# A hybrid decoder step on one core: a first stage of six column tiles with its first rows in single transfers, and a tail that adds the residual on TensorE

## The chip, the core and the metric

The kernel runs on one core of a Trainium2 chip. The metric is device time in microseconds of one execution; lower is better. A time of a kernel is the median of several runs. Besides these runs there is one profiled execution, and every row below is from that one.

The core has TensorE (PE in the rows; its weight load is PEld), VectorE (DVE), ScalarE (ACT), GpSimd (POOL) and SyncE (SP). Each works through its own queue in order. Transfers are issued here from the queues of SP, ACT and POOL.

## The reference

One layer of a hybrid decoder on 280 token columns: 16 meta tokens, 256 prompt tokens and 8 running sequences with one new token each. All data is fp32. Cut to its frame:

```python
u = rmsnorm(h, pre_mix_g)
mix, conv, ssm, ret = mixers(u, ...)     # u @ w_in, conv, Mamba-2 heads, retention heads
h = h + rmsnorm(mix @ w_out, post_mix_g)
f = rmsnorm(h, pre_ffn_g)
f = (silu(f @ w_gate) * (f @ w_up)) @ w_down
h = h + rmsnorm(f, post_ffn_g)           # y_prompt, y_sample
```

`rmsnorm` is x * rsqrt(mean(x*x) + eps) * g. The model width is 2048, or 16 tiles of 128 rows. The outputs are the new h and the new convolution, SSM and retention states.

## The kernel before

Tokens lie on the free axis and features on the partitions, so a projection is a product of 128x128 weight blocks with the 280 (later 264) token columns. To get fp32 accuracy from the faster fp32r mode, weights and activations are split into a high part rounded to fp32r and a low remainder. A block then takes three matmuls (`three`, L129 to L133): high by high, high by low, low by high.

Weights stream in chunks of eight blocks, 512 KB each (`Stream.block`, L112 to L125). SP issues the load into `raw`, four buffers; ScalarE casts to `hi` (L122) and VectorE subtracts to get `lo` (L123), three buffers each. The first chunk is cut in four.

The first stage, `gemm("xb", uin0, ..., outer=4)` at L336, runs with the row tile k outside and four column tiles inside: dt, two tiles of B and the first of C. Each has its own PSUM bank. While it runs, `prep` (L163 to L178) brings in the rows of x on the same SP queue, two at a time (the first two apart), multiplies them by the norm weight `g_pre` from the parameter table `pps`, splits them into `uh` (ScalarE) and `ul` (VectorE, L171), squares them (ScalarE) and adds the squares into `xsum` on GpSimd (L178). The parameter table comes by ScalarE's queue. Nine dummy matmuls (`WARM`) run before the first data is there.

When the stage ends, `const_loads` loads the constants from GpSimd's queue; this is paced by a tiny copy that reads the `ul` of row 11. Then `token_norms` sums `xsum` over the partitions (`pr`, L208) and makes the norm `rbc` on ScalarE and VectorE. Every finished column tile is scaled by it out of PSUM; dt goes through some twenty VectorE operations (`do_dt`), the others through the convolution (`do_xbc`, three VectorE operations L321 of 304 columns each). Column tiles 4 to 12 follow one by one, with k inside. After tiles 7, 8 and 9 a further piece of `do_dt` runs: its transposes, the cumulated decay `lcd`, which is written to DRAM and read back into all partitions as four tiles `lcb` (L293 to L296), and the differences `wj` that read these (L304). The projections k, q, v, z, g, the output projection `o`, the two FFN gemms `f` and `d` follow.

The tail: gemm `d` leaves 16 rows `p` (times the norm weight) and sums of squares; `rstds` makes the norm from them with an fp32 ones-matmul (L638) and ScalarE's Ln and Exp. Then for each of eight pairs of rows one multiplication by the norm (L895) and one addition of the residual `hr` (L903), shared between VectorE and GpSimd, and one store (L904), alternating between SP and ScalarE. `hr` comes back from DRAM in eight loads issued behind gemm d.

The framework puts the instructions of every queue in order before the run: it plays the program through with its own estimates of durations and takes the ready instruction of highest priority. Priority is program order; `tc.high_priority(offset=n)` moves an instruction up by n, and `keep_in_program_order` fixes its place. The order stays, whatever the run's own durations are.

Of the kernel before, what the change touches and what calls it, by code (L numbers as in the profile page):

```python
# [7 lines left out]
F32 = mybir.dt.float32  # L8
F32R = mybir.dt.float32r
# [38 lines left out]
WARM = 9  # L48
OUTF = 6


@with_exitstack
def hybrid_step(ctx: ExitStack, tc: tile.TileContext, wall, xT, pp, cc, dmask, cs, convst, ssm, ret,
# [32 lines left out]

    pps = cp.tile([P, NPP], F32, name="pps")
# [41 lines left out]
    def three(ps, xhi, xlo, first, last):  # L129
        hi, lo = stream.block()  # L130
# [27 lines left out]
    xs = [slot(f"x{i}") for i in range(4)]  # L158
    uh = [slot(f"uh{i}", dt=F32R) for i in range(4)]
    ul = [slot(f"ul{i}", dt=F32R) for i in range(4)]  # L160
    xsum = slot("xsum", NA, 2)

    def prep(k):  # L163
        i, j = divmod(k, 4)
        with tc.high_priority(offset=1500):
            for q in (j, j + 1):
                if k == 0 or q == j:
                    n = 1 if k == 0 else 2
                    nc.sync.dma_start(xs[i][:, q:q + n, :], xT[:, 4 * i + q:4 * i + q + n, :])
                A.activation(uh[i][:, q, :], xs[i][:, q, :], AF.Copy, scale=par("g_pre", 4 * i + q))  # L170
                V.scalar_tensor_tensor(ul[i][:, q, :], xs[i][:, q, :], par("g_pre", 4 * i + q),  # L171
                                       uh[i][:, q, :].bitcast(F32), MULT, SUB)
            if k == 0:
                A.activation(xsum, xs[i][:, j:j + 2, :], AF.Square)
            else:
                sq = slot(f"xq{k}", NA, 2)
                A.activation(sq, xs[i][:, j:j + 2, :], AF.Square)
                G.tensor_tensor(xsum, xsum, sq, ADD)  # L178

    ready = set()  # L180

    def uin0(k, n):
        if k % 2 == 0 and k not in ready:
            ready.add(k)
            prep(k)
        return uin(k, n)

    def uin(k, n):
        i, j = divmod(k, 4)
        return uh[i][:, j, NA - n:NA], ul[i][:, j, NA - n:NA]  # L190
# [26 lines left out]

    def pinned(out, in_):
        tc.keep_in_program_order(G.dma_start(out, in_))
# [660 lines left out]
    o2 = [slot(f"p{i}", NO) for i in range(4)]  # L880
    ev, sums = ev_norm(o2, "g_pffn")
# [3 lines left out]
    hrs = []  # L885
    for k in range(0, KT, 2):
        hr = slot(f"hr{k}", NO, 2)
        load(hr, hd[:, k:k + 2, :])
        hrs.append(hr)
    pool_mul, pool_add = (7,), (0, 2, 4, 7)  # L890

    def scaled(n):
        ok = o2[n // 2][:, 2 * (n % 2):2 * (n % 2) + 2, :]
        e = G if n in pool_mul else V
        e.tensor_tensor(ok, ok, rstd.unsqueeze(1).to_broadcast([P, 2, NO]), MULT)  # L895

    scaled(7)
    for n in range(8):
        ok = o2[n // 2][:, 2 * (n % 2):2 * (n % 2) + 2, :]
        if n < 7:  # L900
            scaled(n)
        e = G if n in pool_add else V
        e.tensor_tensor(ok, ok, hrs[n], ADD)  # L903
        (nc.sync if n % 2 == 0 else nc.scalar).dma_start(yT[:, 2 * n:2 * n + 2, :], ok)  # L904
# [49 lines left out]
def _layout(i):  # L954
# [4 lines left out]
    first = np.concatenate([np.tile(dt, (1, 8)), bb, cm[:, :128]], 1)  # L959
    wo, wd = i["w_out"][0], i["w_down"][0]  # L960
    gu = np.stack([i["w_gate"][0].reshape(DM, FT, P), i["w_up"][0].reshape(DM, FT, P)], 2).reshape(DM, 2 * DFF)
    seq = [_blocks(first, 1), _blocks(np.concatenate([cm[:, 128:], xx], 1)), _blocks(k), _blocks(q), _blocks(v),
           _blocks(z), _blocks(g), _blocks(wo[:, :512], 1), _blocks(wo[:, 512:]), _blocks(gu[:, :P * OUTF], 1),
           _blocks(gu[:, P * OUTF:]), _blocks(wd)]
    wall = np.concatenate(seq, 0)
    wall = np.ascontiguousarray(wall.reshape(-1, CB, P, P).transpose(0, 2, 1, 3)).reshape(-1, P, CB * P)
    xtok = np.concatenate([i["meta_tokens"], i["x_prompt"][0], i["x_sample"][:, 0]], 0)
# [16 lines left out]
    return [wall, xT, pp, c, d, cs, convst, ssm, ret]  # L984
# [31 lines left out]
```

## Time and profile before

| | us |
|---|---|
| median of 3 runs | 1280.14 |
| lowest, highest | 1277.64, 1282.41 |
| the profiled execution | 1281.71 |
| its span in the profile | 1279.9 |

The span is the part of the profiled execution from its first to its last instruction; 1.8 us lie around it. The profiled execution took 1.57 us more than the median. PE carries 98% of the span, and the chain of work that ended last lies on PE for 95%. A matmul row's duration contains the time in which its columns drain while the next is already streaming in, so the distance between two starts is what one more matmul costs. The clock column is the granted clock of TensorE: 1.00 is 2.4 GHz and 0.50 is 1.2 GHz.

### The profile page before, as it was taken

What the parts mean: (1) busy time and instruction counts of PE and PEld (TensorE: products, weight loads), DVE (VectorE), ACT (ScalarE), POOL (GpSimd) and SP (SyncE); (2) the same over time, 40 slices, a digit from 0 to 9 for tenths busy, and PEclk for the clock granted to TensorE, in tenths of its full rate; (3) what the DMA queues carried; (4) which work ended last, traced back from release to release, by engine and by line L of the source; (5) the groups of instructions that cost most, each with busy time, mean ns of one, the idle gap of its engine ahead of it and who ended that gap; (6) DMA issues with size and microseconds to landing.
All of it is one profiled execution on the core that took longest, in us unless ns stands there. A gap on an engine that the chain in (4) does not pass through costs nothing.

```text
span 1279.9 us, 24519 instructions
## 1 busy us (share of the span) xinstructions
PE 1254.4 (98%) x10078; PEld 1240.9 (97%) x10078; DVE 821.3 (64%) x1247; ACT 607.8 (47%) x826; POOL 153.1 (12%) x218
## 2 busy tenths in 40 slices
PE   8989999999999999999999999999999999999994
PEld 7989999999999999999999999999999999999994
DVE  7978779984775458566666666666666544444445
ACT  6665434445854446544444444444444433333331
POOL 3320001100001221101110110101101000000013
PEclk9999999999999999999999999999999999999997
DMA  8656347774466556577677766767676555555562
GB/s 271 206 190 215 121 147 260 273 260 144 136 214 230 182 180 217 183 244 245 229 236 247 246 231 231 248 215 248 214 247 229 183 181 181 182 182 181 181 223 93
DMA packets 74768, 266.41 MB, mean 208 GB/s; under 512 B 8528, under 2 KB 9440, under 8 KB 74656
## 3 DMA queue, kind: packets, MB, share of 16 engines
q1 hardware_dynamic: 60192, 214.17, 51.7%
q0 software_dynamic: 13744, 49.52, 10.7%
q8 instruction: 79, 1.29, 0.4%
q10 hardware_dynamic: 720, 1.16, 0.2%
q14 instruction: 33, 0.27, 0.1%
HBM read 246.15 MB, written 18.66 MB: 207 GB/s over the span
## 4 chain that ended last, share of the span: by engine, by line
PE 95%; DMA 2%; DVE 1%; issue 1%; SPq 0%; ACT 0%; POOL 0%; DVEq 0%; ACTq 0%
PE f L131 13%; PE f L133 13%; PE f L132 13%; PE d L132 7%; PE d L131 7%; PE d L133 7%; PE o L131 2%; PE o L132 2%; PE o L133 2%; PE xb L132 1%; PE xb L133 1%; PE xb L131 1%; PE k L131 1%; PE v L131 1%; PE v L132 1%; PE k L132 1%
## 5 line engine op out<-in xcount | busy, mean ns | idle before, releaser
L123 DVE TENSOR_TENSOR lo<-raw,hi 128x1024 fp32r<-128x1024 f32 (+1 forms) x405 | 492.3, 1217 | 357.8 <-ACT hi L122 353.1
L122 ACT CAST hi<-raw 128x1024 fp32r<-128x1024 f32 (+1 forms) x405 | 422.1, 1043 | 601.9 <-PE f L132 191.7
L131 PE MATMUL f<-fh,hi 128*128 128x264 f32 x1408 | 400.6, 285 | 0.0
L133 PE MATMUL f<-fh,lo 128*128 128x264 f32 x1408 | 399.3, 284 | 0.0
L132 PE MATMUL f<-fl,hi 128*128 128x264 f32 x1408 | 398.6, 283 | 0.0
L132 PEld LDWEIGHTS f<-fl,hi 128*128 128x128 f32 x1408 | 264.8, 188 | 0.3 <-issue 0.2
L131 PEld LDWEIGHTS f<-fh,hi 128*128 128x128 f32 x1408 | 264.8, 188 | 0.3 <-DVE f L863 0.2
L133 PEld LDWEIGHTS f<-fh,lo 128*128 128x128 f32 x1408 | 264.6, 188 | 0.0
L132 PE MATMUL d<-al,hi 128*128 128x264 f32 x704 | 200.2, 284 | 0.0
L131 PE MATMUL d<-ah,hi 128*128 128x264 f32 x704 | 199.7, 284 | 0.0
L133 PE MATMUL d<-ah,lo 128*128 128x264 f32 x704 | 199.4, 283 | 0.0
L131 PEld LDWEIGHTS d<-ah,hi 128*128 128x128 f32 x704 | 132.5, 188 | 0.0
L132 PEld LDWEIGHTS d<-al,hi 128*128 128x128 f32 x704 | 132.4, 188 | 0.0
L133 PEld LDWEIGHTS d<-ah,lo 128*128 128x128 f32 x704 | 132.3, 188 | 0.0
L131 PE MATMUL o<-mh,hi 128*128 128x264 f32 x256 | 72.8, 284 | 0.0
L132 PE MATMUL o<-ml,hi 128*128 128x264 f32 x256 | 72.6, 284 | 0.0
L133 PE MATMUL o<-mh,lo 128*128 128x264 f32 x256 | 72.4, 283 | 0.0
L869 POOL COPY pace<-f 128x1 f32<-128x1 f32 x25 | 28.6, 1144 | 362.2 <-DVE f L863 362.2
L858 DVE TENSOR_TENSOR f<-f,rhc 128x264 f32<-128x264 f32 x88 | 37.6, 432 | 49.1 <-PE f L133 48.8
L131 PE MATMUL xb<-uh,hi 128*128 128x280 f32 x208 | 61.8, 299 | 3.1 <-ACT hi L122 3.1
L133 PE MATMUL xb<-uh,lo 128*128 128x280 f32 x208 | 61.1, 297 | 3.4 <-DVE lo L123 3.4
L132 PE MATMUL xb<-ul,hi 128*128 128x280 f32 x208 | 61.7, 297 | 1.2 <-DVE ul L171 1.2
(296 smaller groups left out, 1983.2 us busy)
## 6 DMA issues: line engine op xcount, KB each, us to landing
raw<-in_dram SPq DMA_DIRECT2D x401, 512.0 KB, 3.6
rs<-in_dram POOLq DMA_DIRECT2D x16, 512.0 KB, 5.3
su<-in_dram POOLq DMA_DIRECT2D x16, 512.0 KB, 4.9
out_dram<-su POOLq DMA_DIRECT2D x16, 512.0 KB, 3.9
hb<-in_dram POOLq DMA_DIRECT2D x8, 512.0 KB, 5.9
hu<-in_dram POOLq DMA_DIRECT2D x8, 512.0 KB, 5.1
out_dram<-hu POOLq DMA_DIRECT2D x8, 512.0 KB, 4.1
lcb<-lcd POOLq DMA_DIRECT2D x4, 544.0 KB, 9.1
```

Of the source, the lines that this page charges most:

```text
L122: A.copy(self.hi[:, f:f + w], raw[:, f:f + w])
L123: V.tensor_tensor(self.lo[:, f:f + w], raw[:, f:f + w], self.hi[:, f:f + w].bitcast(F32), SUB)
L131: T.matmul(ps, hi, xhi, start=first, stop=False)
L132: T.matmul(ps, hi, xlo, start=False, stop=False)
L133: T.matmul(ps, lo, xhi, start=False, stop=last)
L858: V.tensor_tensor(t, ps, rhc, MULT)
L869: tc.keep_in_program_order(G.tensor_copy(pace, t[:, 0:1]))
```

## The change

The first stage takes six column tiles at once (dt, two of B, two of C, the first of x) in place of four, with four banks of one PSUM pool and two of the other. The weights are laid out for that.

For its first four row tiles, the 16 norm weights, the 280 columns of x and the six weight blocks lie next to each other in one new input `head`: 1064 numbers per partition and row tile, 545 KB. SP loads each of the four into a buffer of its own; the first in two parts, the first part with the norm weights, x and two blocks (552 numbers, 283 KB). `bring` casts and splits from there.

The other rows of x come from GpSimd's queue, two per load, each load paced by a tiny copy that reads the `ul` of four rows before (for rows 4 to 7, of rows 0 and 1). The squares are summed on VectorE. `WARM` is 7.

In the tail GpSimd does nothing. VectorE multiplies all eight pairs by the norm. For the first four pairs TensorE adds: an fp32 matmul of the identity with the residual opens a bank, another with the scaled row closes it, and ScalarE copies the sum out. VectorE adds the other four pairs. SP issues all stores. The residual comes in four loads that stand ahead of gemm d.

```diff
-WARM = 9
+WARM = 7
+OUTX = 6
+NHEAD = 4
+HX = 16
+HW = HX + NA + OUTX * P
+NPE = 4
...
-                    w = CB * P // (4 if c == 0 else 1)
-                    for f in range(0, CB * P, w):
-                        nc.sync.dma_start(raw[:, f:f + w], wall[c, :, f:f + w])
-                        A.copy(self.hi[:, f:f + w], raw[:, f:f + w])
-                        V.tensor_tensor(self.lo[:, f:f + w], raw[:, f:f + w], self.hi[:, f:f + w].bitcast(F32), SUB)
+                    nc.sync.dma_start(raw, wall[c])
+                    A.copy(self.hi, raw)
+                    V.tensor_tensor(self.lo, raw, self.hi.bitcast(F32), SUB)
...
+    def x_load(k, after):
+        if k % 4 == 0:
+            xs[k // 4] = slot(f"x{k // 4}")
+        pace = cp.tile([P, 1], F32, name=f"pacex{k}")
+        i, j = divmod(after, 4)
+        tc.keep_in_program_order(G.tensor_copy(pace, ul[i][:, j, 0:1].bitcast(F32)))
+        pinned(xs[k // 4][:, k % 4:k % 4 + 2, :], xT[:, k:k + 2, :])
+    heads = []
+    for k in range(NHEAD):
+        heads.append(slot(f"head{k}").rearrange("p a n -> p (a n)"))
+        with tc.high_priority(offset=1500):
+            cut = HX + NA + 2 * P if k == 0 else HW
+            for f0, f1 in ((0, cut), (cut, HW)):
+                if f0 < f1:
+                    tc.keep_in_program_order(nc.sync.dma_start(heads[k][:, f0:f1], head[k, :, f0:f1]))
+    def bring(k):
...
+            if k == 0:
+                V.tensor_copy(hi[:, :cut], w[:, :cut])
+                parts(k, x, g)
+                V.tensor_tensor(lo[:, :cut], w[:, :cut], hi[:, :cut].bitcast(F32), SUB)
...
+            else:
+                A.copy(hi[:, :cut], w)
+                parts(k, x, g)
+                V.tensor_tensor(lo[:, :cut], w, hi[:, :cut].bitcast(F32), SUB)
...
+            x_load(2 * k + NHEAD, k) if k < 2 else None
     def prep(k):
...
+            squares(k, xs[i][:, j:j + 2, :])
+            if k + 4 < KT:
+                x_load(k + 4, k)
...
-    gemm("xb", uin0, KT, NA, 0, 4, ev_first, outer=4, before=const_loads)
-    for m in range(4, 13):
-        gemm("xb", uin, KT, NA, m, m + 1, ev_first, pool=pm if m < 6 else pg)
+    for k in range(KT):
+        ws = bring(k) if k < NHEAD else [None] * OUTX
+        if k >= NHEAD and k % 2 == 0:
+            prep(k)
+        xh, xl = uin(k, NA)
+        for ps, w in zip(pss, ws):
+            three(ps[:, :NA], xh, xl, k == 0, k == KT - 1, w)
+    const_loads()
+    for m, ps in enumerate(pss):
+        ev_first(m, ps[:, :NA])
+    for m in range(OUTX, 13):
+        gemm("xb", uin, KT, NA, m, m + 1, ev_first, pool=pm if m == OUTX else pg)
...
+    for i in range(4):
+        hr = slot(f"hr{i}", NO)
+        load(hr, hd[:, 4 * i:4 * i + 4, :])
...
+    def residual(k):
+        sums_[k] = bank(f"h{k}", NO) if k % 2 else pg.tile([P, 512], F32, name=f"h{k}", tag="g")[:, :NO]
+        T.matmul(sums_[k], ident, hrs[k // 4][:, k % 4, :], start=True, stop=False)
+    for k in range(4):
+        residual(k)
+    for n in range(NPE):
+        scaled(n)
+        for k in (2 * n, 2 * n + 1):
+            ok = o2[k // 4][:, k % 4, :]
+            T.matmul(sums_[k], ident, ok, start=False, stop=True)
+            A.copy(ok, sums_.pop(k))
+        store(n)
+        for k in (2 * n + 4, 2 * n + 5):
+            if k < 2 * NPE:
+                residual(k)
+    for n in range(NPE, 8):
+        scaled(n)
+        ok = pair(o2, n)
+        V.tensor_tensor(ok, ok, pair(hrs, n), ADD)
+        store(n)
```

## Rows read from the trace of the kernel before

**Rows 1.** The page, parts 1 and 5: busy time, and the two operations that prepare weights.

```profile
PE 1254.4 (98%) x10078; PEld 1240.9 (97%) x10078; DVE 821.3 (64%) x1247; ACT 607.8 (47%) x826; POOL 153.1 (12%) x218
L123 DVE TENSOR_TENSOR lo<-raw,hi 128x1024 fp32r<-128x1024 f32 (+1 forms) x405 | 492.3, 1217 | 357.8 <-ACT hi L122 353.1
L122 ACT CAST hi<-raw 128x1024 fp32r<-128x1024 f32 (+1 forms) x405 | 422.1, 1043 | 601.9 <-PE f L132 191.7
```

**Rows 2.** Windows: stretch, length; PE, PEld, DVE, ACT, POOL busy (x); clock; DMA share; GB/s.

```profile
0.00:10.00 10.00, 7.29 (x42) 6.69 (x42) 3.50 (x9) 5.55 (x11) 0.34 (x6) 1.00 0.71 211
10.00:20.00 10.00, 8.12 (x59) 7.71 (x60) 8.58 (x9) 8.85 (x15) 4.52 (x3) 1.00 0.98 358
```

**Rows 3.** Waits of PE over the whole span: total us, times, longest.

```profile
PE xb L133 <- DVE lo L123: 3.4, 1, 3.4
PE xb L131 <- ACT hi L122: 3.1, 2, 2.1
PE xb L132 <- DVE ul L171: 1.2, 2, 0.8
```

**Rows 4.** Timeline, the first data: start us, us, engine line operation.

```profile
3.52 0.53 ACT L170 ACTIVATE uh<-x,pps 128x280 fp32r<-128x280 f32 x1 [1.05 <-DMA pps<-in_dram]
4.55 0.38 PE L131 MATMUL xb<-uh,hi 128*128 128x280 f32 x1
```

**Rows 5.** Timeline of PE, end of the first stage.

```profile
33.10 0.29 PE L132 MATMUL xb<-ul,hi 128*128 128x280 f32 x1
33.23 0.29 PE L133 MATMUL xb<-uh,lo 128*128 128x280 f32 x1
...
35.30 1.10 PE L208 MATMUL pr<-xsum,ones 128*128 128x280 f32 x4
```

**Rows 6.** Timeline, VectorE's remainder of x with GpSimd idle, and with it adding squares.

```profile
9.12 0.93 DVE L171 SCALAR_TENSOR_TENSOR ul<-x,pps,uh 128x280 fp32r<-128x280 f32 x2 [1.36 <-ACT uh L170]
...
21.24 4.03 DVE L171 SCALAR_TENSOR_TENSOR ul<-x,pps,uh 128x280 fp32r<-128x280 f32 x4
```

**Rows 7.** DMA issues of the first 60 us: queue, count, KB each, median us to landing.

```profile
x<-in_dram SPq DMA_DIRECT2D x7, 280.0 KB, 5.6
dms<-in_dram POOLq DMA_DIRECT2D x1, 544.0 KB, 8.2
x<-in_dram SPq DMA_DIRECT2D x2, 140.0 KB, 3.1
```

**Rows 8.** Timeline of the tail.

```profile
1262.69 0.71 PE L638 MATMUL n<-g_pffnq,ones 128*128 128x264 f32 x2
...
1264.40 4.14 DVE L895 TENSOR_TENSOR p<-p,n5r 128x528 f32<-128x528 f32 x3 [1.24 <-ACT n5r L648]
...
1275.48 1.32 DVE L903 TENSOR_TENSOR p<-p,hr 128x528 f32<-128x528 f32 x2
```

**Rows 9.** Line 904, the stores: ns of an issue, first and last start us; landing.

```profile
L904 SPq DMA_DIRECT2D out_dram<-p x4: 332/338/347, 1269.7 to 1276.8; - x4
...
DMA to landing us min/median/max: 2.0/2.1/2.2
```

**Rows 10.** Timelines of VectorE and PE around the reading back of the decay.

```profile
72.44 0.15 DVE L279 COPY rtok<-pk 128x3 f32<-128x3 f32 x1
...
85.74 0.17 DVE L304 TENSOR_TENSOR wj<-lcb,lct 128x12 f32<-128x12 f32 x1 [3.92 <-DMA lcb<-lcd]
...
92.51 0.40 PE L133 MATMUL xb<-uh,lo 128*128 128x280 f32 x1 [3.36 <-DVE lo L123]
```

**Rows 11.** Windows of 1 us, columns as in rows 2.

```profile
94.00:95.00 1.00, 1.00 (x6) 1.00 (x6) 0.96 (x4) 0.65 (x2) 0.56 (x3) 0.50 0.82 291
...
1267.00:1268.00 1.00, 0.00 (x0) 0.00 (x0) 1.00 (x1) 0.00 (x0) 1.00 (x2) 0.54 0.00 0
```

**Rows 12.** Timeline of GpSimd: a pacing copy of the kernel before, and a load behind it.

```profile
31.61 0.40 POOL L224 COPY pace<-ul 128x1 f32<-128x1 f32 x1
31.95 0.70 POOL L219 DMA_DIRECT2D ccs<-in_dram  x1
```

More of the change, by code (lines that the diff above doesn't have):

```diff
@@ L47, with hybrid_step @@
 DECAY_ACT = False
-WARM = 9
+WARM = 7
[3 more added lines that the diff above has]
+HW = HX + NA + OUTX * P
 OUTF = 6
+NPE = 4
 @with_exitstack
-def hybrid_step(ctx: ExitStack, tc: tile.TileContext, wall, xT, pp, cc, dmask, cs, convst, ssm, ret,
+def hybrid_step(ctx: ExitStack, tc: tile.TileContext, head, wall, xT, pp, cc, dmask, cs, convst, ssm, ret,
                 yT, oconv, opssm, opret, osssm, osret):
@@ L85, in load, with pinned @@
         G.dma_start(out, in_)
+    def pinned(out, in_):
+        tc.keep_in_program_order(G.dma_start(out, in_))
     pps = cp.tile([P, NPP], F32, name="pps")
@@ L127, in hybrid_step, with three @@
     stream = Stream()
-    def three(ps, xhi, xlo, first, last):
-        hi, lo = stream.block()
+    def three(ps, xhi, xlo, first, last, w=None):
+        hi, lo = w or stream.block()
         T.matmul(ps, hi, xhi, start=first, stop=False)
@@ L157, in hybrid_step @@
     table("sqrt_and_others")
-    xs = [slot(f"x{i}") for i in range(4)]
     uh = [slot(f"uh{i}", dt=F32R) for i in range(4)]
@@ L161, in hybrid_step, with uin, parts, squares @@
     xsum = slot("xsum", NA, 2)
+    xs = {}
+    def uin(k, n):
+        i, j = divmod(k, 4)
+        return uh[i][:, j, NA - n:NA], ul[i][:, j, NA - n:NA]
+    def parts(k, x, g):
+        i, j = divmod(k, 4)
+        A.activation(uh[i][:, j, :], x, AF.Copy, scale=g)
+        V.scalar_tensor_tensor(ul[i][:, j, :], x, g, uh[i][:, j, :].bitcast(F32), MULT, SUB)
+    def squares(k, x):
+        sq = xsum if k == 0 else slot(f"xq{k}", NA, 2)
+        A.activation(sq, x, AF.Square)
+        if k:
+            V.tensor_tensor(xsum, xsum, sq, ADD)
@@ new lines, in hybrid_step @@
+    hsq = {}
+    def bring(k):
+        t = heads[k]
+        hi = st.tile([P, CB * P], F32R, name=f"hh{k}", tag="hi")
+        lo = st.tile([P, CB * P], F32R, name=f"hl{k}", tag="lo")
+        x, w = t[:, HX:HX + NA], t[:, HX + NA:HW]
+        cut = 2 * P if k == 0 else OUTX * P
+        with tc.high_priority(offset=1500):
+            g = heads[0][:, k:k + 1]
+            if k == 0:
+                V.tensor_copy(hi[:, :cut], w[:, :cut])
+                parts(k, x, g)
+                V.tensor_tensor(lo[:, :cut], w[:, :cut], hi[:, :cut].bitcast(F32), SUB)
+                tc.keep_in_program_order(A.copy(hi[:, cut:OUTX * P], w[:, cut:]))
+                tc.keep_in_program_order(V.tensor_tensor(lo[:, cut:OUTX * P], w[:, cut:],
+                                                         hi[:, cut:OUTX * P].bitcast(F32), SUB))
+            else:
+                A.copy(hi[:, :cut], w)
+                parts(k, x, g)
+                V.tensor_tensor(lo[:, :cut], w, hi[:, :cut].bitcast(F32), SUB)
+            if k % 2 == 0:
+                hsq[k // 2] = xsum if k == 0 else slot(f"xq{k}", NA, 2)
+            A.activation(hsq[k // 2][:, k % 2, :], x, AF.Square)
+            if k == 3:
+                V.tensor_tensor(xsum, xsum, hsq[1], ADD)
+            x_load(2 * k + NHEAD, k) if k < 2 else None
+        return [(hi[:, m * P:(m + 1) * P], lo[:, m * P:(m + 1) * P]) for m in range(OUTX)]
@@ L165, in prep @@
         with tc.high_priority(offset=1500):
[L166 to L190, printed above, removed]
+            for q in (k, k + 1):
+                parts(q, xs[i][:, q - 4 * i, :], par("g_pre", q))
+            squares(k, xs[i][:, j:j + 2, :])
+            if k + 4 < KT:
+                x_load(k + 4, k)
     sxn = cp.tile([P, 64], F32, name="sxn")
@@ L335, in hybrid_step @@
     held = {}
-    gemm("xb", uin0, KT, NA, 0, 4, ev_first, outer=4, before=const_loads)
-    for m in range(4, 13):
-        gemm("xb", uin, KT, NA, m, m + 1, ev_first, pool=pm if m < 6 else pg)
+    pss = [pg.tile([P, 512], F32, name=f"xb{m}", tag="g") if m < 4 else
+           pm.tile([P, 512], F32, name=f"xb{m}", tag="m") for m in range(OUTX)]
+    for k in range(KT):
[10 more added lines that the diff above has]
+        gemm("xb", uin, KT, NA, m, m + 1, ev_first, pool=pm if m == OUTX else pg)
         if 7 <= m < 10:
@@ L884, in hybrid_step, with pair, store @@
     (rstd,) = rstds("n5", [[sums["a"], sums["b"]]], 1.0 / DM, load_table=False)
[L885 to L890, printed above, removed]
-    def scaled(n):
[L893 to L904, printed above, removed]
+    def pair(tiles, n):
+        return tiles[n // 2][:, 2 * (n % 2):2 * (n % 2) + 2, :]
+    def scaled(n):
+        ok = pair(o2, n)
+        V.tensor_tensor(ok, ok, rstd.unsqueeze(1).to_broadcast([P, 2, NO]), MULT)
+    def store(n):
+        nc.sync.dma_start(yT[:, 2 * n:2 * n + 2, :], pair(o2, n))
+    sums_ = {}
+    def residual(k):
[15 more added lines that the diff above has]
+        scaled(n)
+        ok = pair(o2, n)
+        V.tensor_tensor(ok, ok, pair(hrs, n), ADD)
+        store(n)
 def _constants():
```

14 lines of the change are left out of this document (8 added, 6 removed).

## The prediction

> **What bounds the kernel now.** I read the page first: PE is busy for 98% of the span [rows 1], so time can only come from places where PE stands still, or from work that is not PE's. The windows and PE's waits give those places. They are few: all waits within the matmul stream lie in the first 100 us and sum to 7.7 us [rows 3], and after the last matmul 15.5 us pass without PE [rows 8]. In the first two windows PE is busy for 7.29 and 8.12 us of 10, while the transfers run at 211 and 358 GB/s [rows 2]. The change touches the first and the last of these places.
>
> How much the first stage loses: its matmuls start 0.128 us apart when nothing is missing (two neighbours 33.10 and 33.23, [rows 5]). It has 16 row tiles x 4 column tiles x 3 = 192 matmuls, 24.6 us. The next work (`pr`) starts at 35.30 [rows 5], so 10.7 us are lost: 4.55 before the first matmul [rows 4] and 6.1 in gaps. The gaps name their releasers: weights cast late, `ul` late.
>
> The 3.4 us wait for `lo` [rows 3] is of another kind. VectorE stood at `wj`, 3.92 us for its first tile, for the decay read back from DRAM; the next `lo` was queued behind the rest of it, and PE waited 3.36 us for that [rows 10]. PE's granted clock was 0.50 in the stretch after it [rows 11]; 14 matmuls there start about 0.23 us apart in place of 0.13, another 1.5 us.
>
> **The first stage.** Work per row tile grows from 12 to 18 matmuls, 1.54 to 2.30 us; bytes grow from 262 + 143 to 393 + 143 KB. So the demand falls from 263 to 233 GB/s, below the 358 that the second window reached [rows 2]. VectorE's share falls too: `lo` costs 1.22 us per 1024 columns [rows 1], 0.92 us for 768; `ul` costs 0.47 alone and 1.0 while GpSimd adds squares [rows 6]. With the squares on VectorE (560 columns; the tail's additions of 528 columns take 0.66, [rows 8], so 0.70 per two rows, 0.35 per row) a row costs 0.92 + 0.47 + 0.35 = 1.74 of 2.30 us. Before it was 0.61 + 1.0 of 1.54. ScalarE: 0.78 + 0.47 + 0.33 of 2.30. No engine binds once it runs.
>
> The beginning is a chain. The first transfer is 283 KB in place of 140; 140 KB landed after about 3.1 us at the median, the very first a little sooner [rows 7]. At 358 GB/s the further 143 KB take 0.4, so it lands at about 0.74 + 2.7 + 0.4 = 3.8. Before, ScalarE waited until 3.52 for the parameter table [rows 4]; this wait goes, since the norm weight now comes with x. Then `uh` 0.53, `ul` 0.5, `lo` of 256 columns 0.42: the first matmul at 4.4 and an unbroken run from 5.3. Two fewer dummy matmuls uncover nothing, as TensorE waits for data anyway; if the clock were granted later for that, some 15 early matmuls would cost 0.1 us more each, 1.5 us. The rest of row 0 lands 0.7 later, and its `lo` ends near 6.1; row 0 is done at 7.4. Row 1 (545 KB, 1.4 us) lands near 6.0 and needs cast 0.78, `uh` 0.5, `ul` 0.5, `lo` 0.92, so its third matmul can start at 8.8 and the row ends at 10.9. From here on the rows come faster (1.4 to 1.6 us each) than PE takes them (2.30). Lost by then: 10.9 - 2 x 2.30 = 6.3 us, against 10.7. That is a gain of 4.4; I take off 0.6 for small gaps when six tiles are scaled at once and their VectorE operations stand ahead of `lo`. **Gain 3.8 us**; bounds 1 (if the first 2 MB come at the first window's 211 GB/s, rows 0 to 3 arrive 1.2 us apart later each) and 5.
>
> The other rows of x leave SP's queue, so nothing but weights stands there. On GpSimd each load waits for a pacing copy; only the later pairs and the constants are queued behind it. That chain is the one new wait: `ul` of row k, copy 0.40, issue 0.70 [rows 12], landing 5.6 [rows 7], then `uh` and `ul` 1.0, in all 7.7 us for four rows, and PE takes 9.2 for four. It starts 1 us after `ul` of row 0 and hides, with 1.5 us gained per round.
>
> **The middle.** The work is the same, but the scaling of tiles 4 and 5 comes together with the others, and all of it starts later: the stage ends near 35.3 + 12.3 - 3.8 = 43.8 in place of 35.3. The forecast keeps the wait at `wj` with its price (3.36 + 1.5 us): it comes from VectorE's queue holding a `lo` behind an operation on late data, and nothing in the change moves either. It is not excluded that the new order changes it; bounds below.
>
> **The tail.** Before: norm ready at 1264.40, last addition ends 1276.80, last store issued then, end of span 3.1 us later (issue 0.34 and landing 2.1 of it, [rows 9]). VectorE's multiplications took 1.38 each beside GpSimd and its last additions 0.66 alone [rows 8]. After: 8 + 4 = 12 operations on VectorE at 0.66 without GpSimd, 7.9 us, end 1272.3, 4.5 sooner. TensorE: an fp32 matmul of this kind is two records and takes some 0.45 us (four records of `pr` within 0.9, [rows 5]). Four residual matmuls run while ScalarE makes the norm; then 12 remain, each pair of sums with the pair opened behind it 1.8 us, so that the fourth pair is summed at about 1270.6 and copied out by 1271.1 (ScalarE, two copies of 0.4 a pair). On SP the four stores of VectorE's pairs stand behind that one: five stores of 270 KB from 1271.1 on need 5 x 0.7 and 1.4 until the last has landed, so 1276.0 and an end near 1276.5. **Gain 3.4 us.** Bounds: 4.8 if only VectorE's end counts, none if the clock is lost: it fell to 0.54 in the fourth microsecond after the last matmul [rows 11]. In the change TensorE goes on at once, so I expect it to hold; at 1.2 GHz the 16 matmuls take 0.9 each, the fourth pair is done near 1278, and the end is near 1283, 3 us later than now. The earlier residual loads lie under gemm d and cost nothing; four raw buffers cover them.
>
> **Sum.** 3.8 + 3.4 = 7.2 us off the profiled 1281.71: 1274.5. The profiled execution lies 1.57 above the median, so the median would be 1272.9; I say 1273.
>
> **Rivals.** (1) The wait at `wj` goes or shrinks, because VectorE, with more queued, comes to it only when the data is there: another 4.9, 1268. For it: VectorE has no slack left there. Against: the order is fixed by estimates, and they were short before. Chance 0.13. (2) The first stage stays bound by arrivals: early transfers at 211 GB/s, or the GpSimd chain. With the 8.2 us of the one large GpSimd load before [rows 7] a round is 10.3, 1.1 over PE's 9.2 per four rows, and the first round, begun at 5.3, is late by 2: some 4 us, and the stage's gain is gone: 1277, at worst 1279. Chance 0.18. (Beside this rival stands a rule of the Trainium skill, "SBUF — State Buffer", section "SBUF: two separate sides": a load issued from GpSimd's queue gets its descriptors from GpSimd, which is locked out of a shared port while VectorE runs an fp32 copy within SBUF, so the load belongs on SP's or ScalarE's queue. By it this part of the change goes the wrong way and 1277 would be the time. The slow GpSimd load of rows 7 is in line with it, but the constants came together there, and no row separates the two.) (3) The tail at the low clock: -3.8 + 3, 1279. Chance 0.07. (4) Slower than before: the dt chain comes later and VectorE waits longer. `rtok` was reached at 72.44 [rows 10], 36 us behind the stage's end, on a VectorE that was busy almost throughout. With the same work the new one comes to it near 80 to 82, 8 to 9 us later, while PE is 3.8 earlier. If `wj` keeps its place against the `lo` it stands before, VectorE waits 12 us longer and PE with it: -7.2 + 12, and 1285 with more of the low clock. It decides from 7 us of additional wait on. Against it: the order is laid out anew, with this delay in it. Chance 0.1. The forecast as such has 0.52.
>
> **How the numbers follow.** What a measurement of this kernel can tell from no change is about 0.5%, 6.4 us: below 1273.7 is faster, above 1286.5 slower. The forecast lies close to the first line; I give it 0.34 faster and 0.18 same. Rival 1 is faster (0.13); 2 is same but for 0.02; 3 is same; 4 is half slower, with 0.02 more for gaps further down. So 0.49, 0.44, 0.07. The range goes from 1267 (both gains at their bounds, or rival 1) to 1281 and leaves out the worse part of rival 4.
>
> **What would show it.** `pr` (or what follows the first stage) near 44.9 in place of 48.7 for the same work; the first matmul at 4.4; no wait of `uh` for x beyond row 1; 0.66 for every VectorE operation in the tail, the last addition near 1264.4 + 7.9 after the shift, the clock 1.00 in those 6 us; a wait of `wj` and one of PE for `lo` of 3 to 4 us. The prediction is wrong if rows of x come later than PE needs them, if PE's wait behind `wj` is above 7 us, or if PE stands at new places in the projections k and q.

## The result, and the profile after

The changed kernel takes 1270.37 us (median, 1270.15 to 1271.08), the kernel before, with one run more than in its own table, 1279.37 us (1277.64 to 1282.41). The ratio is 0.9928 [0.9908, 0.9948]: 0.7% faster, outside the 0.5% that can be told from no change. The profiled execution took 1271.08, its span is 1269.3: 10.6 us below the profiled 1281.71 and 1279.9 of before. The forecast was 7.2 below.

Marks in the two traces show where the 10.6 us lie. The first `pr` matmul ends the first stage; `cb`, the first product of the SSM part, ends the projections of x; f and d are taken from their first to their last `hi` by `hi` matmul.

| stretch | before, us | after, us | gain |
|---|---|---|---|
| start to `pr`; before with tiles 4 and 5 added (96 x 0.128 = 12.3) | 35.30 + 12.3 = 47.6 | 45.23 | 2.4 |
| `pr` to `cb`; before without those two tiles | 106.29 - 47.6 = 58.7 | 98.66 - 45.23 = 53.4 | 5.3 |
| `cb` to f | 487.5 - 106.3 = 381.2 | 480.0 - 98.7 = 381.3 | -0.1 |
| gemm f | 1005.3 - 487.5 = 517.8 | 999.2 - 480.0 = 519.2 | -1.4 |
| gemm d | 1261.6 - 1005.7 = 255.9 | 1255.3 - 999.6 = 255.7 | 0.2 |
| last matmul of d to the end | 1279.9 - 1261.6 = 18.3 | 1269.3 - 1255.3 = 14.0 | 4.3 |

Half of the gain lies in the second line, where the forecast had none. Both columns are single executions, and the one of before lies 2.3 us above its kernel's median; e1 and e4 below show how much of the 5.3 us varies. PE's waits in the changed kernel, in the columns of [rows 3]:

```profile
PE xb L137 <- ACT uh L175: 1.3, 1, 1.3
PE xb L139 <- DVE lo L129: 0.5, 1, 0.5
PE xb L138 <- DVE ul L176: 0.3, 1, 0.3
```

Of the 7.7 us in the matmul stream 2.1 are left, and the 3.4 us wait for `lo` is gone. The windows of the start, columns as in [rows 2]:

```profile
0.00:10.00 10.00, 7.29 (x37) 6.54 (x38) 3.69 (x8) 5.42 (x10) 1.50 (x10) 1.00 0.77 269
10.00:20.00 10.00, 10.00 (x80) 10.00 (x79) 9.44 (x14) 7.75 (x14) 4.01 (x4) 1.00 0.92 331
```

The second window is full where it was busy for 8.12 us. The first is as empty as before, and the timeline of the changed kernel says why:

```profile
3.70 0.53 ACT L175 ACTIVATE uh<-head 128x280 fp32r<-128x280 f32 x1 [1.24 <-DMA head<-in_dram]
...
4.28 0.83 PE L137 MATMUL xb<-uh,hh 128*128 128x280 f32 x2
...
7.05 0.29 PE L139 MATMUL xb<-uh,hl 128*128 128x280 f32 x1
7.35 0.83 ACT L220 CAST hh<-head 128x768 fp32r<-128x768 f32 x1 [2.00 <-DMA head<-in_dram]
...
8.66 0.65 PE L137 MATMUL xb<-uh,hh 128*128 128x280 f32 x3 [1.32 <-ACT uh L175]
...
9.64 0.40 PE L138 MATMUL xb<-ul,hh 128*128 128x280 f32 x1 [0.33 <-DVE ul L176]
```

Row 0 is done at 7.2, but row 1 has landed only just before 7.35, and cast and `uh` of it take until 8.6.

The windows around `wj`, the first two lines from the kernel before, then the same two of the changed kernel:

```profile
80.00:90.00 10.00, 9.14 (x71) 8.91 (x69) 4.34 (x18) 5.25 (x7) 1.89 (x6) 1.00 0.91 317
90.00:100.00 10.00, 7.49 (x46) 7.50 (x47) 8.40 (x14) 8.27 (x13) 0.56 (x3) 0.83 0.56 158
```

```profile
80.00:90.00 10.00, 10.00 (x78) 9.61 (x77) 8.80 (x20) 6.76 (x15) 2.90 (x9) 1.00 0.37 115
90.00:100.00 10.00, 10.00 (x78) 9.89 (x77) 6.44 (x15) 4.83 (x10) 4.39 (x10) 1.00 0.96 344
```

71 + 46 matmuls in 20 us became 78 + 78. VectorE's queue in this place, first before (its `lo` and `wj` from 80 to 92 us; the first `wj`, at 85.74, is in [rows 10]), then after:

```profile
80.59 1.23 DVE L123 TENSOR_TENSOR lo<-raw,hi 128x1024 fp32r<-128x1024 f32 x1 [0.58 <-ACT hi L122]
...
87.45 0.17 DVE L304 TENSOR_TENSOR wj<-lcb,lct 128x12 f32<-128x12 f32 x1
...
91.14 0.17 DVE L304 TENSOR_TENSOR wj<-lcb,lct 128x12 f32<-128x12 f32 x1 [2.31 <-DMA lcb<-lcd]
91.23 1.22 DVE L123 TENSOR_TENSOR lo<-raw,hi 128x1024 fp32r<-128x1024 f32 x1
```

```profile
82.94 0.16 DVE L324 COPY rtok<-pk 128x3 f32<-128x3 f32 x1
...
87.87 1.22 DVE L129 TENSOR_TENSOR lo<-raw,hi 128x1024 fp32r<-128x1024 f32 x1
...
90.79 1.22 DVE L129 TENSOR_TENSOR lo<-raw,hi 128x1024 fp32r<-128x1024 f32 x1
94.89 0.17 DVE L349 TENSOR_TENSOR wj<-lcb,lct 128x12 f32<-128x12 f32 x1 [2.88 <-DMA lcb<-lcd]
...
96.53 0.22 DVE L349 TENSOR_TENSOR wj<-lcb,lct 128x12 f32<-128x12 f32 x1
...
97.11 1.21 DVE L129 TENSOR_TENSOR lo<-raw,hi 128x1024 fp32r<-128x1024 f32 x1
98.87 0.17 DVE L349 TENSOR_TENSOR wj<-lcb,lct 128x12 f32<-128x12 f32 x1 [0.54 <-DMA lcb<-lcd]
```

Before, three `wj` stand between two `lo`, and these lie 10.6 us apart (80.59 to 91.23), while a chunk of eight blocks lasts PE only 24 x 0.128 = 3.1 us. PE waited for 3.36 us of the 10.6, so it could go on for about 7.3 us from one `lo` to the next with what it had. After, the first `wj` still waits 2.88 us, but a `lo` now stands between the second and the third `wj`. The largest distance is 6.3 us (90.79 to 97.11), less than those 7.3, and PE does not wait.

The tail of the changed kernel, and its line of stores:

```profile
1258.21 3.80 DVE L953 TENSOR_TENSOR p<-p,n5r 128x528 f32<-128x528 f32 x6 [1.33 <-ACT n5r L704]
...
1262.19 1.94 PE L971 MATMUL h<-p,ccs 128*128 128x264 f32 x8
1262.84 1.71 ACT L972 COPY p<-h 128x264 f32<-128x264 f32 x4 [0.96 <-PE h L971]
...
1264.41 1.31 DVE L980 TENSOR_TENSOR p<-p,hr 128x528 f32<-128x528 f32 x2
```

```profile
L956 SPq DMA_DIRECT2D out_dram<-p x8: 332/333/408, 1260.6 to 1265.8; - x8
```

VectorE's operations take 0.63 (3.80 / 6) and 0.66 each where those of before took 1.38 beside GpSimd [rows 8]. TensorE's share is copied out by 1264.55 (1262.84 + 1.71); VectorE ends at 1265.72, and the last store is issued at 1265.8 (before: 1276.8, [rows 9]).

### The profile page after: what moved, and what is told of

Same layout as the page of the kernel before. It is cut to its first block, busy times and chain, and to the rows that moved or that the text cites. A ratio compares the mean times of both kernels' runs of the same rounds, so it can differ in the third digit from the quotient of the medians.

```text
span 1269.3 us, 24558 instructions
## 1 busy us (share of the span) xinstructions
PE 1260.7 (99%) x10106; PEld 1246.2 (98%) x10106; DVE 813.1 (64%) x1255; ACT 605.5 (48%) x830; POOL 138.7 (11%) x214
## 4 chain that ended last, share of the span: by engine, by line
PE 96%; DVE 1%; DMA 1%; ACT 1%; issue 0%; POOL 0%; SPq 0%; DVEq 0%; ACTq 0%
PE f L138 14%; PE f L137 13%; PE f L139 13%; PE d L138 7%; PE d L137 7%; PE d L139 7%; PE o L137 2%; PE o L138 2%; PE o L139 2%; PE xb L139 2%; PE xb L138 1%; PE xb L137 1%; PE k L137 1%; PE v L137 1%; PE k L138 1%; PE v L138 1%
## 5 line engine op out<-in xcount | busy, mean ns | idle before, releaser
L129 DVE TENSOR_TENSOR lo<-raw,hi 128x1024 fp32r<-128x1024 f32 x399 | 488.1, 1224 | 357.7 <-ACT hi L128 353.3
L128 ACT CAST hi<-raw 128x1024 fp32r<-128x1024 f32 x399 | 418.6, 1050 | 590.5 <-PE f L138 191.9
L139 PE MATMUL xb<-uh,lo 128*128 128x280 f32 x184 | 54.1, 294 | 0.5 <-DVE lo L129 0.5
L137 PE MATMUL xb<-uh,hi 128*128 128x280 f32 x184 | 53.9, 293 | 0.0
L138 PE MATMUL xb<-ul,hi 128*128 128x280 f32 x184 | 53.8, 293 | 0.0
```

The costliest lines, as they stand in the source:

```text
L128: A.copy(self.hi, raw)
L129: V.tensor_tensor(self.lo, raw, self.hi.bitcast(F32), SUB)
```

## The experiments

The table collects the marks of their profiled executions; "tail" is from the first of the norm's ones-matmuls to the end of the span, "f" the length of gemm f as above.

| kernel | median, us | ratio to before | `pr` | `pr` to `cb`, like for like | f | tail |
|---|---|---|---|---|---|---|
| before | 1279.37 | 1 | 35.30 (47.6) | 58.7 | 517.8 | 17.9 |
| after | 1270.37 | 0.9928 [0.9908, 0.9948] | 45.23 | 53.4 | 519.2 | 13.6 |
| e1, tail alone | 1276.30 | 0.9963 [0.9947, 0.9979] | 34.82 (47.1) | 55.2 | 517.7 | 13.5 |
| e2, all but the tail | 1275.17 | 0.9963 [0.9949, 0.9976] | 44.30 | 53.4 | 519.2 | 18.1 |
| e3, six tiles alone | 1274.15 | 0.9948 [0.9929, 0.9967] | 45.10 | 53.5 | 517.7 | 18.0 |
| e4, `wj` later | 1276.13 | 0.9966 [0.9956, 0.9976] | 35.60 (47.9) | 53.5 | 517.8 | 17.9 |
| e5, VectorE adds all | 1272.82 | 0.9945 [0.9928, 0.9961] | 44.93 | 53.5 | 519.2 | 15.6 |
| e6, x on SP | 1270.04 | 0.9921 [0.9902, 0.9941] | 46.10 | 53.4 | 518.7 | 13.8 |
| e8, row 1 in two transfers | 1271.70 | 0.9939 [0.9921, 0.9957] | 44.04 | 53.5 | 519.7 | 13.5 |
| e10, six tiles and the tail | 1270.28 | 0.9924 [0.9909, 0.9938] | 45.22 | 53.5 | 517.8 | 13.5 |
| e12, after again | 1270.12 | 0.9927 [0.9910, 0.9943] | 44.10 | 53.4 | 519.2 | 13.6 |
| e13, other places | 1274.01 | 0.9960 [0.9947, 0.9974] | 47.75 | 53.4 | 519.8 | 13.6 |

**The two ends apart.** e1 is the kernel before with the new tail, e2 the changed kernel with the old one.

```diff
 # e1, on before:  the tail of the diff, with
+NPE = 4
 # e2, on after:   the eight loads of hr behind gemm d and the loop
 #                 with pool_mul, pool_add = (7,), (0, 2, 4, 7) put back
```

> The kernel before with the tail of the change alone (residual loaded ahead of gemm d, GpSimd out, TensorE adding four of eight pairs, all stores on SP). Theory: the tail is worth the 4.4 us that the two profiles show from the norm's end to the span's end, so 4.4 us off the kernel before; VectorE's operations in the tail take 0.63 each, and the first stage and PE's 3.4 us wait for lo behind wj stay as before. Rival: the 1.4 us that gemms f and d took longer in the changed kernel (738.0 to 739.4 us between the same two points) are a cost of the tail part, through the earlier loads of the residual; then only 3.0 us come off, and f and d are slower here too.

> The changed kernel with the tail of before. Theory: 2.4 us from the first stage and 5.2 us from PE's wait behind wj and the low clock after it, 7.6 us off the kernel before, or 6.2 if gemms f and d are slower here as in the changed kernel; the tail lasts 15.5 us from the norm's end as before. Rival: the parts need each other and this one alone gives clearly less than 6 us.

Measured: e1 1276.30 beside 1280.61, a gain of 4.3; e2 1275.17, 5.4 below the same. The 6.2 us expected of e2 were not reached at the median. Together they give 9.7, as much as the whole change in e12's set of runs (1279.86 to 1270.12); in the first set the whole change gave 9.0. The tail's length falls from 17.9 to 13.5 us in e1 as in the changed kernel, so it needs nothing of the first stage. One warning lies in e1: its first stage and its `wj` are those of before, and yet its profiled execution lost 3.5 us less in the middle (55.2 for 58.7). PE waited for `lo` 1.1 us at the longest there:

```profile
PE xb L134 <- DVE lo L124: 1.4, 2, 1.1
```

```profile
80.12 1.23 DVE L124 TENSOR_TENSOR lo<-raw,hi 128x1024 fp32r<-128x1024 f32 x1 [0.58 <-ACT hi L123]
...
88.46 1.22 DVE L124 TENSOR_TENSOR lo<-raw,hi 128x1024 fp32r<-128x1024 f32 x1
```

So the wait behind `wj` is not a fixed 3.4 us. With the order of before, the four `lcb` landed after 7.7 us at the median here and after 9.1 in the profile of before, and the two `lo` around `wj` lay 8.3 us apart in place of 10.6.

**Six tiles alone.**

```diff
-    gemm("xb", uin0, KT, NA, 0, 4, ev_first, outer=4, before=const_loads)
-    for m in range(4, 13):
-        gemm("xb", uin, KT, NA, m, m + 1, ev_first, pool=pm if m < 6 else pg)
+    gemm("xb", uin0, KT, NA, 0, 6, ev_first, outer=6, before=const_loads)
+    for m in range(6, 13):
+        gemm("xb", uin, KT, NA, m, m + 1, ev_first, pool=pm if m == 6 else pg)
```

> The kernel before with six column tiles in the first stage and the weights laid out for that, nothing else (x and the parameter table as before, squares on GpSimd, nine dummy matmuls). Theory A on the wait behind wj: it went because six tiles move the order of VectorE's queue, so that a lo stands between the second and the third wj where before three wj stood ahead of the next lo; here that order is there too, so PE waits under 0.5 us for lo and the clock stays 1.00: 4.9 us off. Rival B: the decay came back sooner (7.9 in place of 9.1 us) because of the other transfers; then PE's wait of 3 to 4 us is still here. On the first stage: by the demand argument (18 matmuls a row in place of 12) half of the gaps go, 2 to 3 us off; by the rival that the single head transfers carry the gain, none. In all 5 to 8 us off by theory A, 0 to 3 by the rivals.

Measured: `pr` at 45.10 and `cb` at 98.57, within 0.13 us of the changed kernel's 45.23 and 98.66. Without any `head` transfer, with x on SP's queue, the parameter table on ScalarE's and the squares on GpSimd, the whole gain of the first stage is there, and the wait behind `wj` is gone as well (PE waits for `lo` 0.4 us at the longest). VectorE's queue in e3 has the order of the changed kernel:

```profile
90.69 1.22 DVE L123 TENSOR_TENSOR lo<-raw,hi 128x1024 fp32r<-128x1024 f32 x1
95.09 0.17 DVE L304 TENSOR_TENSOR wj<-lcb,lct 128x12 f32<-128x12 f32 x1 [3.18 <-DMA lcb<-lcd]
...
97.09 1.23 DVE L123 TENSOR_TENSOR lo<-raw,hi 128x1024 fp32r<-128x1024 f32 x1
```

The median is even 1.0 us below e2's. For the first stage this is in line with the forecast's lower demand, 233 GB/s in place of 263; no run varies the demand alone. What the rest of the change does at the start is within what the start varies by: `pr` comes between 44.1 and 46.1 in five profiled executions with `head` loads (after, e2, e5, e12 and e6), and at 45.10 and 45.22 in e3 and e10.

**`wj` moved, and nothing else.** The pieces of `do_dt` run behind tiles 7, 8 and 11 in place of 7, 8 and 9.

```diff
-        if 7 <= m < 10:
+        if m in (7, 8, 11):
```

> The kernel before with one step moved: the last piece of the dt work (transposes of the decay and the four wj) is traced behind column tile 11 in place of 9, so that three more lo stand ahead of the first wj on VectorE. Theory: the wait of PE for lo (3.4 us) and the low clock behind it (1.5 us) go, 4.9 us off the kernel before, with the first stage and the tail unchanged. Rival: the wait only moves, to the operations that read the decay later, and less than 1.5 us come off.

Measured: 4.4 us at the median against 4.9 expected for this wait, and 53.5 us in the middle, as in all builds with six tiles. From 20 us on PE has no wait for `lo`. VectorE's timeline of e4 from 85 us on shows the order:

```profile
86.63 1.23 DVE L123 TENSOR_TENSOR lo<-raw,hi 128x1024 fp32r<-128x1024 f32 x1 [0.29 <-ACT hi L122]
...
89.74 1.23 DVE L123 TENSOR_TENSOR lo<-raw,hi 128x1024 fp32r<-128x1024 f32 x1 [0.48 <-ACT hi L122]
...
91.33 0.25 DVE L304 TENSOR_TENSOR wj<-lcb,lct 128x12 f32<-128x12 f32 x2
...
93.47 0.17 DVE L304 TENSOR_TENSOR wj<-lcb,lct 128x12 f32<-128x12 f32 x1 [1.36 <-DMA lcb<-lcd]
```

Three `wj` (two at 91.33, one at 91.93) find their data and the fourth waits 1.36 us, which the `lo` ahead of it cover. The four `lcb` landed after 8.5 us at the median, not far from the 9.1 of before, so the order in VectorE's queue is enough to remove the loss. In the builds with six tiles the first `wj` still waits 2.0 to 3.2 us, and the `lo` around it lie 6.0 to 6.7 us apart, under the 7.3 that PE goes on for. There the `lcb` also landed sooner, after 7.6 to 8.3 us; with the landing of before, about 1 us later, the distance would be 7 to 7.7 (an estimate from these numbers), so PE would wait 0.4 us at most. The new order by itself thus removes nearly all of the loss; a sooner landing by itself does not, as e1 shows, which still lost 1.7 us with the old order (55.2 less 53.5).

**Who adds in the tail.**

```diff
-NPE = 4
+NPE = 0
...
-    for k in range(4):
+    for k in range(2 * min(NPE, 2)):
         residual(k)
```

> The changed kernel with VectorE adding all eight pairs, TensorE none. Theory: the tail then hangs on VectorE alone, 16 operations of 0.63 us, 10.1 us in place of 12 x 0.63 = 7.6, so 2.5 us more than the changed kernel, about 1272.9; taking GpSimd out gives the rest of the tail's 4.4 us. Rival: the stores on one queue set the end, so the adding engine matters little and it is under 1 us slower.

Measured: 2.5 us more than the changed kernel, tail 15.6. The last addition of e5:

```profile
1258.10 1.33 DVE L953 TENSOR_TENSOR p<-p,n5r 128x528 f32<-128x528 f32 x2 [1.25 <-ACT n5r L704]
...
1266.77 1.33 DVE L980 TENSOR_TENSOR p<-p,hr 128x528 f32<-128x528 f32 x2
```

It ends 10.0 us after VectorE's first operation of the tail; in the changed kernel that is 7.5. So of the tail's 4.3 us TensorE's additions bring 2.0 to 2.5. The other 2.3 (17.9 to 15.6) belong to the rest of the new tail: GpSimd out, all stores on SP, the residual loaded ahead. No run takes these three apart; the shorter VectorE operations speak for the first.

**x from SP.** The loads of x without pacing on SP's queue.

```diff
-        tc.keep_in_program_order(G.tensor_copy(pace, ul[i][:, j, 0:1].bitcast(F32)))
-        pinned(xs[k // 4][:, k % 4:k % 4 + 2, :], xT[:, k:k + 2, :])
+        nc.sync.dma_start(xs[k // 4][:, k % 4:k % 4 + 2, :], xT[:, k:k + 2, :])
```

> The changed kernel with the later rows of x issued by SP without pacing copies, among the weights. Theory: the chain on GpSimd did not bind (PE waits under 0.5 us for rows 4 to 15 in the changed kernel), so the first stage ends within 1 us of 45.4. Rival: GpSimd's queue was needed to keep x from delaying weights; then PE waits for hi or lo in row 4 and later, 2 us or more. On gemm f: if its slower pace comes from where the buffers lie in memory (the six pacing copies have a tile each ahead of all other pools), 2479 matmul starts in 300 us are back here; if it comes from the head transfers or the layout of the weights in DRAM, it stays at 2471.

Measured: 1270.04, the changed kernel's time; `pr` 0.9 later, f 0.5 shorter. The rival's wait for `hi` or `lo` from row 4 on is not there. The later `pr` has another source: in this execution, the slowest of the four, PE stood from 7.5 to 9.1 before row 1, and from 11.08 on 15 matmuls started 0.23 us apart, which costs 1.5 us. The granted clock was 0.50 there:

```profile
12.00:13.00 1.00, 1.00 (x6) 1.00 (x6) 1.00 (x3) 1.00 (x3) 0.00 (x0) 0.50 1.02 418
```

The chain on GpSimd is slower than forecast at single links and costs nothing that the times show. Its first, third and fourth pacing copies in the changed kernel:

```profile
4.94 0.18 POOL L190 COPY pacex<-ul 128x1 f32<-128x1 f32 x1 [4.06 <-DVE ul L176]
...
14.15 1.12 POOL L190 COPY pacex<-ul 128x1 f32<-128x1 f32 x1 [3.82 <-DVE ul L176]
...
17.91 2.19 POOL L190 COPY pacex<-ul 128x1 f32<-128x1 f32 x1 [2.17 <-DVE ul L176]
```

**No `head`, new tail.** e10 is e3 with the tail of e1.

> The kernel before with six column tiles alone (as in e3_six_only) and the new tail; no head transfers, x on SP, squares on GpSimd, nine dummy matmuls. Theory: head transfers and x on GpSimd's queue bring nothing net, since e3_six_only already ended its first stage at 45.3 as the changed kernel did; then this is 4.4 us under e3_six_only, 1269.7, equal to the changed kernel or up to 1.4 us faster, as gemm f is not slower here (2479 matmul starts in 300 us, against 2471 in the changed kernel). Rival: the head transfers are worth what I forecast, 1 to 2 us, hidden by the spread of single profiles; then this is 1 to 2 us slower than the changed kernel's 1270.4.

Measured: 1270.28 beside 1280.15, level with the changed kernel. So the four `head` transfers, x on GpSimd and the squares on VectorE pay nothing at the end. They gain up to 1 us at the start (`pr` at 44.10 in e12 beside 45.10 in e3) and lose 1.4 us in f.

**Row 1 in two transfers.** The wait of 1.32 us for row 1 should go if its first two blocks come first.

```diff
-            cut = HX + NA + 2 * P if k == 0 else HW
+            cut = HX + NA + 2 * P if k < 2 else HW
```

with the casts of row 1 split in the same way and their order fixed.

> The changed kernel with row 1 of the first stage brought in like row 0: its transfer in two parts (norm weights, x and two blocks first), the first two blocks cast on VectorE, the order of these operations pinned. Theory: in the changed kernel PE stands 1.3 us before row 1 and 0.3 within it because 545 KB must have landed (7.33) and 768 columns must be cast before its first matmul; half the bytes and a cast of 0.3 beside uh bring its first matmul from 8.7 to about 7.5, so PE waits 1 us less and the kernel is 0.5 to 1.2 us faster than the changed one. Rival: row 2 becomes the next wait, since it lands when it did (row 2's third matmul could start at 11.5 at the earliest), and nothing is gained.

Measured: nothing gained; 1271.70 is 1.6 above e12 on the same chip. `pr` comes at 44.04 beside 44.10 in e12, so the loss is not in the first stage: of the 0.9 us between the two profiled executions 0.5 lie in f and 0.4 between `cb` and f. That the first stage gained nothing has two reasons. First, e12 is the changed kernel itself, and in this execution PE did not wait for row 1 at all, because its load landed by 6.12 and not by 7.35:

```profile
6.12 0.83 ACT L220 CAST hh<-head 128x768 fp32r<-128x768 f32 x1 [0.75 <-DMA head<-in_dram]
```

Second, in e8 eight of the matmuls before row 2 start 0.23 us apart, some 0.8 us:

```profile
6.14 0.43 PE L138 MATMUL xb<-ul,hh 128*128 128x280 f32 x1
6.38 0.44 PE L137 MATMUL xb<-uh,hh 128*128 128x280 f32 x1
6.61 0.43 PE L138 MATMUL xb<-ul,hh 128*128 128x280 f32 x1
```

This is the distance that the kernel before shows behind the `wj` wait at a granted clock of 0.50 [rows 11]. It is also the distance in e6 at 0.50. The profile's clock column, however, reads 1.00 in these first microseconds, so that it is the lower level here is an inference from the distance.

**The slower gemm f.** Four kernels went after the 1.4 us. e9 adds six one-column tiles to e3 (moving the addresses of the constants' pool), e11 adds four slots to e3 at the start, e12 is the changed kernel once more, and e13 is the changed kernel with 24 slots taken first, so that f's operands, counted through the ring of 27 slots, lie where they lay before (the change takes 3 slots more ahead of them).

```diff
 # e9, on e3
+    for i in range(6):
+        G.memset(cp.tile([P, 1], F32, name=f"pad{i}"), 0.0)
 # e11, on e3
+    for i in range(4):
+        G.memset(slot(f"dm{i}")[:, 0, 0:1], 0.0)
 # e13, on after, ahead of css
+    for i in range(24):
+        G.memset(slot(f"dm{i}")[:, 0, 0:1], 0.0)
```

> e3_six_only with six more tiles of one column in the pool that lies ahead of the others, each set to zero once by GpSimd at the start; no other change. If gemm f's pace comes from where the buffers lie, it falls from 2479 to about 2471 matmul starts in 300 us here, 1.4 us for f; if not, it stays at 2479 and the run is like e3_six_only.

> e3_six_only with four more buffers of the large pool taken at the start and given back at once (each touched by one small write of GpSimd), as the four head buffers are, so that later tiles lie in other buffers. If gemm f's pace in the changed kernel (2471 matmul starts in 300 us in place of 2479) comes from which buffers its tiles lie in, it moves here too; if it stays at 2479, that cause falls and the layout of the weights in DRAM or the chunk count is left.

> The changed kernel once more, on the same chip as e8_row1_split, so that the two can be set side by side; 1270.4 by all theories. On the spread: the kernel before ranged over 5 us in each set of runs, the versions without the wait behind wj over 1 to 2; by the theory that this wait makes the spread, these runs lie within 2 us.

> The changed kernel, with 24 one-column tiles taken from the ring of 27 slots ahead of everything else. The changed kernel takes three more slots before gemm f's operands than the kernel before, so fh and fl lie three places further on in the ring; with 24 more they lie where they lay in the kernel before (3 + 24 = 27). Theory (places): gemm f runs at the old pace, 517.8 us from its first to its last matmul in place of 519.2, about 2479 starts in 600 to 900 us; the time is 1.4 us lower, near 1268.9. Rival (something else of the head transfers' build, the chunk sequence or the code): f stays at 519 us or above, at most 2474 starts, and the time stays near 1270.2. The first stage should not change by more than 0.5 us by either.

Measured, in matmuls of f that the window from 600 to 900 us counts: before 2479, e9 2479, e11 2483, after and e12 2471 both, e13 2468 (f 519.8 us). e9 took 1274.07 and e11 1274.62, in one execution each. Line 137 of the changed kernel and line 131 of before, each over gemm f (ns of one: least, median, most; first and last start):

```profile
L137 PE MATMUL f<-fh,hi x1408: 278/283/682, 480.0 to 999.2; 128*128 128x264 f32 x176
```

```profile
L131 PE MATMUL f<-fh,hi x1408: 278/283/687, 487.5 to 1005.3; 128*128 128x264 f32 x176
```

PE is busy throughout, and neither trace has a wait or a distance between two starts above 0.13 us in this stretch: the mean distance is 0.1215 us in place of 0.1211, evenly. The new tail (e1, e10), the constants' addresses (e9) and the place of f's operands in the ring (e13) are excluded as the cause. All builds with `head` loads have it (2468 to 2474), no other does (2479 to 2483). Two rivals are left untested: the layout of the weights in DRAM, and the buffers of the weights. Four `head` tiles take the place of three chunks in the three `hi` and `lo` buffers, so from then on each chunk lies in another of these buffers than before. The cause stays open.

e13 also shows what the start is worth. In it SP issues a 512 KB load of weights ahead of the first `head` part, which lands 4.2 us after its issue where the changed kernel's took 2.9. The dummy matmuls are through before it:

```profile
6.06 0.83 PE L139 MATMUL xb<-uh,hh 128*128 128x280 f32 x2 [1.64 <-ACT uh L177]
...
9.84 0.43 PE L139 MATMUL xb<-uh,hh 128*128 128x280 f32 x1
10.07 0.43 PE L140 MATMUL xb<-ul,hh 128*128 128x280 f32 x1
```

PE starts 1.8 us later (6.06 for 4.28), 15 matmuls from 7.04 on then run 0.23 us apart (15 x 0.10 = 1.5), row 1 is there in time for that, and `pr` comes at 47.75: 2.5 us later than in the changed kernel's first profile, 3.6 later than in e12's, against at most 0.5 expected. The time is 3.9 us above e12's, which ran on another chip.

## Why the prediction was right, and where it was not

It held in its sign and its range, 1267 to 1281, though its likeliest time was 2.6 us too high. Of the two profiles' difference it had 7.2 of 10.6. That the time fell into the range was in part luck: the forecast missed 5.3 us at `wj` and 0.9 in the tail, and came near because it also had 1.4 too much in the first stage and did not have the 1.4 lost in f. By its steps:

- **First stage, 3.8 forecast, 2.4 measured.** The mechanism, lower demand per matmul and an unbroken run after the first rows, agrees with the trace: PE is busy throughout from 10 to 20 us. The first matmul came at 4.28 (4.4 forecast) and row 0 ended at 7.2 (7.4). The mis-sized term is the landing of row 1: forecast at 6.0, by adding 1.4 us for its bytes to row 0's landing; it landed at 7.3, 1.3 later. Its third matmul started at 9.88 in place of 8.8, and row 1 ended at 11.7 in place of 10.9, which is 0.8 of the missing 1.4. The rest are two late `lo`, near 29 and 33 us, that cost 1.1 us where 0.6 was taken off for gaps. The forecast priced a queued transfer by its bytes alone; in this trace three `head` loads took 6.5 us at the median from issue to landing. But the landing varies: in e12, the same kernel, they took 5.5, row 1 landed by 6.1 and `pr` came at 44.10, a gain of 3.5. The cast of row 1 began between 6.1 and 7.8 in the five executions named above, so 6.0 was the early end. e3 shows that the six tiles carry a gain of 2.5 alone, which the forecast did not separate. (The forecast puts `pr` at 44.9 in place of 48.7 in one place; its own sums, 43.8 and 47.6, are what 45.23 compares with.)
- **Dummy matmuls, nothing forecast.** Right in the changed kernel's profile, but not in every execution: the slow early matmuls that were priced at 1.5 (15 of them) number three in e12, seven in e2, eight in e8 and 15 in e6 and e13. No run varies `WARM` alone, and e3, with nine dummies, has five, so it is not shown that the two fewer are the cause.
- **The wait at `wj`, kept by the forecast, is gone: 5.3.** This is the step that failed. The forecast said that nothing in the change moves either `lo` or the operation on late data. But the six tiles change VectorE's queue: tiles 4 and 5 are scaled with the first four, and a `lo` now stands between the second and the third `wj`, where three `wj` stood ahead of the next `lo`. Rival 1 named the outcome and its price, 4.9, with a chance of 0.13, but by another way: VectorE would come to `wj` only when the data is there. It came to `rtok` at 82.94 (80 to 82 forecast) and still waited 2.88. e4 shows with one moved step that the order is enough to remove the wait: it gained 4.4 at the median. The size, 5.3, belongs to the one profile of before with its late landing; in e1's profile the old order cost 1.7.
- **The tail, 3.4 forecast, 4.3 measured.** VectorE's end was right: 7.9 us forecast from the norm to the last addition, 7.5 measured (1258.21 to 1265.72). The term that was wrong is SP's queue: the fourth TensorE pair was expected at 6.7 us after the norm, with four stores behind it. It was copied out at 6.3 us, when VectorE still had most of its last two additions ahead, and only the stores of these two stood behind its own, which was issued at 1264.6. The last store was issued 0.1 us after VectorE's end, so the end hangs on VectorE as in the upper bound. (The forecast has that bound as 4.8; its own ends, 1276.8 and 1272.3, make it 4.5. And its 15.5 us without PE run from the norm's end; from the end of the last matmul, 1263.4, they are 16.5.) The clock's part held: TensorE was granted 1.00 in every 2 us window from 1258 to 1266.
- **Gemm f, nothing forecast, 1.4 lost.** No row of before bore on it.
- **Rival 2** (arrivals or the GpSimd chain) falls: the window from 10 to 20 us is full, and e6 without that chain has the same time. Six loads from GpSimd's queue landed after 5.6 us at the median, as SP's did before [rows 7]. The rule cited beside this rival, of the Trainium skill, "SBUF — State Buffer", section "SBUF: two separate sides", starves such loads while VectorE runs an fp32 copy within SBUF. That case did not arise: behind the cast at 3.70 VectorE ran only operations with two inputs in SBUF while the loads were issued (5.1 to 26.9 us), so the forecast should not have priced the rule at 1277, and the loads' 5.6 us are no test of it. The same section says that a VectorE operation with two SBUF inputs holds up a GpSimd operation that reads SBUF. The trace agrees with that: the copy of 2.19 us above ends at 20.1, with VectorE's `lo` of 18.83 to 20.05. **Rival 3** falls with the clock, **rival 4** with `wj`: its condition, a later `rtok`, came true, 10.5 us later than before, and PE had no wait there.

## What to carry to other kernels

Before pricing a stall as fixed, list what stands ahead of and behind the late read on its engine: moving one step by two column tiles (e4) gave 4.4 us, as much as the whole new tail. Take a change apart before keeping all of it: the six tiles, by their lower demand and by the order behind them, and the new tail make the whole gain (e10), and the elaborate first transfers beside them add nothing at the end. Take the landing of a large transfer that queues behind another as a range from several executions: here the second row was cast from 6.1 to 7.8 us, and its bytes over the bandwidth gave 6.0.

## What the runs showed of the hardware

- The same stream of matmuls runs at a slightly different pace in different builds: 2468 to 2483 matmuls of f in a window of 300 us, repeated by a second execution of the same kernel (2471 and 2471), with no wait in the trace. That is up to 0.5% of gemm f (517.2 us in e11, 519.8 in e13).
- A stall that waits for a transfer also widens the runs: the kernel before spreads over 5 to 7 us in its sets of 4 to 18 runs, those without the stall over 0.5 to 2.6 us (e3, e2). e4, which differs from before by the moved step alone, spreads over 1.2 us in eight runs.
- A copy of one column on GpSimd took 0.18 us at 4.94 and 2.19 us at 17.91 beside VectorE's operations with two inputs.
- The start is sensitive: with a weight load ahead of the first 283 KB, in the one profile of e13, the first stage ended 2.5 us later than in the first profile of the changed kernel, about as much as the new stage had gained.
- The same 545 KB load, third in SP's queue, landed 4.4 us after its issue in one execution (e12) and 5.7 in another of the same kernel (after).
- Matmuls of 280 columns started 0.23 us apart at a granted clock of 0.50 (e6, 12 to 13 us) and 0.13 at 1.00.
